# Where tiles begin in their partition: small working tiles moved to a pool at the end

## The chip, the core and the metric

The kernel runs on one core of one Trainium2 chip. TensorE (PE in the rows, its weight loads PEld), VectorE (DVE), ScalarE (ACT), GpSimd (POOL) and SyncE (SP, which issues the DMAs) work side by side and wait for each other by semaphores. The metric is the device time of one execution in microseconds, the median of three runs.

## The reference

Two layers over 512 positions of width 1024, all in float32. Layer 0 mixes tokens by gated linear attention in chunks of 64, layer 1 by a short gated convolution; each is followed by a causal convolutional feed-forward network of width 2816, and a last RMS norm ends it:

```
for i in range(DEPTH):                                   # DEPTH = 2
    h = rmsnorm(x, norm_mix_g[i])
    x = x + (gla_mixer(h, ...) if i % 2 == 0 else short_conv_mixer(h, ...))
    h = rmsnorm(x, norm_ffn_g[i])
    x = x + conv_ffn(h, ...)     # up = causal_dwconv(h @ w_up); (silu(a) * u) @ w_down
return rmsnorm(x, final_norm_g)
```

## The kernel before

x lies transposed in SBUF: eight tiles of 128 channels by 512 positions. To keep float32 accuracy every large product is three matmuls of float32r parts (`mm3`, L176 to L181): each operand is split into a rounded high part and the rest as a low part, and high by high, high by low and low by high are added in PSUM. One matmul keeps a 128x128 block as its stationary operand, which a weight load brings in, and streams the other, moving, operand of 128x512 past it. Mostly the weights are stationary (`wh`, `wl`, split from the loaded `wr`) and the activations move (`xh`, `xl` for a layer's input, `g0h` to `g21l` for the feed-forward's middle). For v (`v_unit`, L345) it is the other way: the weights move and blocks of `xh`, `xl` are stationary. The last output tile is done in halves of 256 positions (`dn7a`, `dn7b`), with its weights split into tiles that the layer's input has left (`wlast`).

Weights come in 201 units of up to 512 KB; each is loaded (L85), its high part is copied by ScalarE (L105), its low part is subtracted by VectorE (L106), and TensorE takes it in the order of the program. Nothing is scheduled by a planner: each engine runs its instructions in program order.

Tiles lie in pools, one pool behind the other in every partition, in the order in which the pools are opened (L38 to L42): const, wraw, wsp, work, big. Within a pool the tiles lie in the order in which they are first made, and a tile smaller than 32 bytes takes 32 (`rl0` and `rl1` take 64 each, for two buffers). Starts are counted in bytes from the beginning of the partition:

| tiles | first start before | rest after division by 512 |
|---|---|---|
| `ident`, `onesr`, `causal` (const) | 35328 | 0 |
| `wr`; `wh`, `wl` (wraw, wsp) | 36864; 53248 | 0 |
| `acc`, `sq` (also `sh`, `sl`), `r`, `u` (work) | 77824 | 0 |
| `ends`, `wst` (work, 8 and 3 numbers, made in `decays`) | 94208 | 0 to 160 |
| `c1`, `c0` (work) | 94400 | 192 |
| `rl0`, `rl1` (work, 2 numbers) | 102592 | 192, 256 |
| all of big: `als`, `xh`, `xl`, `g*`, `y*`, `s*`, `v`, `qs`, `ks`, `zw`, `alr`, `wlast`, ... | 102720 | 320 |

The tiles of big are 2048 bytes each, so all of them have rest 320; so have their blocks of 128 columns, which are 512 bytes. The small tiles ahead of them are what sets that rest.

## Time and profile before

| | |
|---|---|
| median of 3 runs | 1128.9 us (1128.77 to 1128.91) |
| the profiled execution | 1128.92 us, of it 1127.2 us from the first instruction to the last |
| TensorE busy | 1117.7 us, 5020 matmul records |
| VectorE, ScalarE busy | 681.5 us, 459.7 us |
| mean granted TensorE clock | 0.998 |

The duration of one matmul in the profile (near 0.39 us for 512 columns) is from its start to the end of its results and overlaps the next one's. What a matmul costs in a stream is the distance from its start to the next start. The chain of waits gives that well: it lists stretches of work by start, length and number of instructions, and length by number is the distance.

### The profile page before, as it was taken

To read this page: it belongs to the slowest core of one execution; us is meant where nothing else is said; L and a number is where in the kernel's file an instruction comes from. 1 tells how busy PE (TensorE), PEld (TensorE's weight loads), DVE (VectorE), ACT (ScalarE), POOL (GpSimd) and SP (SyncE) were. 2 spreads that over 40 slices of the span, in tenths; PEclk is the share of its full clock that TensorE was granted. 3 is DMA by queue.
4 is the path that set the end of the run, shared out by engine and by line. 5 is a ranking of instruction groups with operands and counts; after the bars stand their busy time and mean duration, and the time that the engine had idled before them with its cause. 6 is when DMAs were issued, how large, how long until landed. Compare 5 with 4: busy or idle time off the path is not lost.

```text
span 1127.2 us, 12505 instructions
## 1 busy us (share of the span) xinstructions
PE 1117.7 (99%) x5020; PEld 922.1 (82%) x5020; DVE 681.5 (60%) x854; ACT 459.7 (41%) x610; POOL 5.1 (0%) x18
## 2 busy tenths in 40 slices
PE   9999999999999999999999999999999999999997
PEld 7888888888888888888888888888888888888887
DVE  6864675597777777433336555558777777753232
ACT  6565664354444444322232222334444444432241
POOL 1000000000000000000000000000000000000000
PEclk9999999999999999999999999999999999999999
DMA  7231223222333333233333322222333323232312
GB/s 256 76 108 61 66 65 113 94 94 94 94 95 100 102 97 89 84 103 98 95 101 99 98 94 94 94 94 94 95 101 104 94 94 94 89 101 87 97 58 75
DMA packets 33183, 108.14 MB, mean 96 GB/s; under 512 B 3619, under 2 KB 6435, under 8 KB 33125
## 3 DMA queue, kind: packets, MB, share of 16 engines
q1 hardware_dynamic: 33124, 107.34, 30.3%
q8 instruction: 39, 0.64, 0.2%
q14 instruction: 20, 0.16, 0.0%
HBM read 105.23 MB, written 2.10 MB: 95 GB/s over the span
## 4 chain that ended last, share of the span: by engine, by line
PE 99%; DVE 0%; DMA 0%; ACT 0%; SPq 0%; issue 0%; DVEq 0%
PE up L181 43%; PE dn L181 20%; PE v L181 4%; PE g L181 4%; PE scb L181 4%; PE scc L181 4%; PE so L181 4%; PE go L181 4%; PE scu L181 4%; PE k L181 2%; PE q L181 2%; PE dn7b L181 1%; PE dn7a L181 1%; PE o L402 1%; PE o L404 0%; DMA x<-in_xT 0%
## 5 line engine op out<-in xcount | busy, mean ns | idle before, releaser
L105 ACT CAST wh<-wr 128x1024 fp32r<-128x1024 f32 (+3 forms) x201 | 204.8, 1019 | 381.8 <-PE dn L181 114.5
L106 DVE TENSOR_TENSOR wl<-wr,wh 128x1024 fp32r<-128x1024 f32 (+3 forms) x201 | 237.9, 1184 | 159.9 <-ACT wh L105 155.7
L181 PE MATMUL up<-xh,wh 128*128 128x512 f32 x704 | 277.5, 394 | 0.0
L181 PE MATMUL up<-xh,wl 128*128 128x512 f32 x704 | 276.0, 392 | 0.0
L181 PE MATMUL up<-xl,wh 128*128 128x512 f32 x704 | 273.3, 388 | 0.0
L181 PEld LDWEIGHTS up<-xh,wl 128*128 128x128 f32 x704 | 132.2, 188 | 30.9
L181 PEld LDWEIGHTS up<-xl,wh 128*128 128x128 f32 x704 | 132.2, 188 | 29.4
L181 PEld LDWEIGHTS up<-xh,wh 128*128 128x128 f32 x704 | 132.5, 188 | 26.3
L494 DVE TENSOR_TENSOR u<-up,r 128x512 f32<-128x512 f32 x88 | 60.2, 688 | 75.7 <-PE up L181 75.7
L242 DVE SCALAR_TENSOR_TENSOR c<-u,ffcw,c 128x510 f32<-128x510 f32 x88 | 65.8, 750 | 2.8
L241 DVE SCALAR_TENSOR_TENSOR c<-u,ffcw,c 128x511 f32<-128x511 f32 x88 | 65.4, 746 | 0.8 <-ACT c L240 0.8
L240 ACT ACTIVATE c<-u,ffcw 128x512 f32<-128x512 f32 x88 | 63.3, 723 | 2.5 <-DVE u L494 2.1
L496 ACT ACTIVATE c<-c 128x512 f32<-128x512 f32 x44 | 27.8, 632 | 83.6 <-DVE c L242 83.6
L497 DVE TENSOR_TENSOR c<-c,c 128x512 f32<-128x512 f32 x44 | 30.5, 693 | 1.6 <-ACT c L496 0.2
L234 DVE RECIPROCAL r<-r 128x512 f32<-128x512 f32 x8 | 26.8, 3351 | 4.7 <-ACT r L233 4.7
L217 ACT ACTIVATE sq<-x 128x512 f32<-128x512 f32 x34 | 21.0, 623 | 12.6 <-DVE x L531 10.9
L181 PE MATMUL g<-xh,wh 128*128 128x512 f32 x64 | 25.9, 404 | 0.0
L181 PE MATMUL v<-wh,xh 128*128 128x512 f32 x64 | 25.7, 401 | 0.0
L207 DVE SCALAR_TENSOR_TENSOR xl<-x,small,xh 128x512 fp32r<-128x512 f32 x32 | 23.6, 746 | 3.2 <-ACT xh L206 3.1
L181 PE MATMUL v<-wl,xh 128*128 128x512 f32 x64 | 25.3, 396 | 0.0
L181 PE MATMUL v<-wh,xl 128*128 128x512 f32 x64 | 25.3, 396 | 0.0
L181 PE MATMUL scu<-xh,wh 128*128 128x512 f32 x64 | 25.2, 394 | 0.0
(798 smaller groups left out, 1864.2 us busy)
## 6 DMA issues: line engine op xcount, KB each, us to landing
wr<-in_w_up SPq DMA_DIRECT2D x88, 512.0 KB, 3.4
wr<-in_w_dn SPq DMA_DIRECT2D x32, 512.0 KB, 3.5
wr<-in_w_sc SPq DMA_DIRECT2D x24, 512.0 KB, 3.3
wr<-in_w_dn SPq DMA_DIRECT2D x16, 384.0 KB, 3.1
wr<-in_w_v SPq DMA_DIRECT2D x8, 512.0 KB, 3.4
wr<-in_w_g SPq DMA_DIRECT2D x8, 512.0 KB, 3.3
wr<-in_w_go SPq DMA_DIRECT2D x8, 512.0 KB, 3.4
wr<-in_w_so SPq DMA_DIRECT2D x8, 512.0 KB, 3.4
```

The lines of the kernel that those rows point to most:

```text
L105: S.copy(hh, r[:, c:e])
L106: V.tensor_sub(ll, r[:, c:e], hh.bitcast(F32))
L181: PE.matmul(out, lhsT=a, rhs=b, start=first and i == 0, stop=last and i == 2)
L207: V.scalar_tensor_tensor(l, x[k], col(gi, k), h.bitcast(F32), op0=ALU.mult, op1=ALU.subtract)
L217: S.activation(sq, x[k], AF.Square)
L234: V.reciprocal(r, r)
L240: S.activation(c, u, AF.Copy, scale=cw[:, 2:3])
L241: V.scalar_tensor_tensor(c[:, 1:], u[:, :T - 1], cw[:, 1:2], c[:, 1:], op0=ALU.mult, op1=ALU.add)
L242: V.scalar_tensor_tensor(c[:, 2:], u[:, :T - 2], cw[:, 0:1], c[:, 2:], op0=ALU.mult, op1=ALU.add)
L494: V.tensor_mul(u, ups[i], r)
L496: S.activation(cs[0], cs[0], AF.Silu)
L497: V.tensor_mul(cs[1], cs[1], cs[0])
```

## The change

The tiles `ends`, `wst`, `rl0` and `rl1` are made in a pool of their own, `tiny`, which is opened behind big. Nothing else differs.

```
     big = ctx.enter_context(tc.tile_pool(name="big", bufs=1))
+    tiny = ctx.enter_context(tc.tile_pool(name="tiny", bufs=2))
...
-    def wk(name, shape=(P, T), dt=F32, bufs=2, tag=None):
-        return work.tile(list(shape), dt, tag=tag or name, name=name, bufs=bufs)
+    def wk(name, shape=(P, T), dt=F32, bufs=2, tag=None, pool=work):
+        return pool.tile(list(shape), dt, tag=tag or name, name=name, bufs=bufs)
+    def tk(name, shape, bufs=2):
+        return wk(name, shape, bufs=bufs, pool=tiny)
...
-        ends = wk("ends", (P, NPAIR, 2))
+        ends = tk("ends", (P, NPAIR, 2))
...
-        wst[h] = wk("wst", (P, NPAIR - 1), bufs=4)
+        wst[h] = tk("wst", (P, NPAIR - 1), bufs=4)
...
-        rt = wk(f"rl{th}", (P, 2))
+        rt = tk(f"rl{th}", (P, 2))
```

In the program that is built from it, `c1` and `c0` begin at 94208 and big at 102400, so that every tile of big has rest 0 instead of 320; `ends`, `wst` and `rl` lie from 225280 on. `const`, `wraw`, `wsp` and `acc` to `u` stay where they are. Of what matmuls read, `ones` (one column, at 16544, rest 160) and `rl` still do not begin at a multiple of 512. Every engine has the same instructions in the same order with the same waits as before; only addresses differ.

## Rows read from the trace of the kernel before

**Rows 1.** Page: busy time by engine; the chain that ended last, by engine.
```profile
PE 1117.7 (99%) x5020; PEld 922.1 (82%) x5020; DVE 681.5 (60%) x854; ACT 459.7 (41%) x610; POOL 5.1 (0%) x18
...
PE 99%; DVE 0%; DMA 0%; ACT 0%; SPq 0%; issue 0%; DVEq 0%
```

**Rows 2.** Waits of TensorE: for whom, us in total, times, longest.
```profile
PE warm L68 <- DVE warm L56: 1.5, 1, 1.5
PE sums L552 <- DVE sq L546: 1.0, 1, 1.0
PE rb L565 <- DVE rl L559: 0.6, 1, 0.6
```

**Rows 3.** Busy time and granted clock in one stretch of the feed-forward's first product.
```profile
225.00:455.00 230.00, 230.00 (x1006) 188.80 (x1006) 171.34 (x214) 101.74 (x131) 0.00 (x0) 1.00 0.30 95
```

**Rows 4.** Chain of waits: start us, us, what; weights stationary, activations moving.
```profile
16.27 10.99 PE q L181 x48
...
169.60 43.95 PE go L181 x192
...
225.00 230.73 PE up L181 x1008
455.73 120.85 PE dn L181 x528
...
576.58 5.49 PE scc L181 x24
```

**Rows 5.** The same chain: v, first and last stretch, with weights moving and activations stationary.
```profile
56.33 22.39 PE v L181 x96
...
104.14 5.60 PE v L181 x24
```

**Rows 6.** The same chain: sums of squares, `sh`, `sl` moving, `onesr` stationary.
```profile
27.26 0.46 PE sums L231 x2
...
103.68 0.47 PE sums L231 x2
...
763.83 0.46 PE sums L231 x2
```

**Rows 7.** The same chain: low-rank gate, `als` stationary, `xh`, `xl` moving.
```profile
10.08 0.45 PE al L262 x2
...
11.22 0.45 PE al L262 x2
...
13.53 0.46 PE al L262 x2
...
14.68 0.45 PE al L262 x2
```

**Rows 8.** The same chain: the last output tile's halves, 256 columns, `wlast` stationary.
```profile
1100.77 7.90 PE dn7a L181 x66
...
1113.96 3.60 PE dn7b L181 x30
```

**Rows 9.** The same chain: the four products for the keys.
```profile
33.21 5.50 PE k L181 x24
...
38.95 5.59 PE k L181 x24
...
44.77 5.51 PE k L181 x24
...
50.51 5.59 PE k L181 x24
```

**Rows 10.** The same chain: float32 matmuls of 256 columns, for the states.
```profile
85.53 0.86 PE kva L386 x4
```

**Rows 11.** Page, costliest groups: two VectorE products of the same shape.
```profile
L494 DVE TENSOR_TENSOR u<-up,r 128x512 f32<-128x512 f32 x88 | 60.2, 688 | 75.7 <-PE up L181 75.7
...
L497 DVE TENSOR_TENSOR c<-c,c 128x512 f32<-128x512 f32 x44 | 30.5, 693 | 1.6 <-ACT c L496 0.2
```

## The prediction

> **What bounds the kernel now.** I read the page's busy times and its chain first. TensorE is busy for 1117.7 of 1127.2 us, and the chain that ended last is TensorE for 99% [rows 1]. The waits of TensorE come next: the three that matter add up to 3.1 us, one at the start and two at the tail [rows 2], so no other engine, queue or transfer sets the pace between. [...] So only one thing can move this time by much: the distance from one matmul's start to the next.

> The chain of waits gives that distance, as length by number. In the products with stationary weights it is 230.73 us / 1008 = 228.9 ns, and the same in 120.85 / 528, in 43.95 / 192, in 10.99 / 48 and in 5.49 / 24 [rows 4]. A column seems to take one cycle: the last tile's 120.0 ns for 256 columns and the gate's 226.3 ns for 512 [rows 7, 8] are 106.3 ns apart, and 256 cycles at 2.4 GHz are 106.7. By that 512 columns are 213.3 ns, and 15.6 ns of every matmul are something else. In v it is 22.39 / 96 = 233.2 ns, and 5.60 / 24 = 233.3 in the last of its five stretches [rows 5]. There are then at least two paces for the same shape, and what differs between these stages is which operand begins at which rest modulo 512 (and in which pool it lies). With the table of starts:

> - moving 320, stationary 0 (most of the kernel): 228.9 ns [rows 4];
> - moving 0, stationary 320 (v): 233.2 ns [rows 5];
> - moving 0, stationary 0 (sums): eight pairs, five of 0.46 and three of 0.47 us, 3.71 / 16 = 231.9 ns [rows 6];
> - moving 320, stationary 320 (the gate): 0.45, 0.45, 0.46 and 0.45 us for pairs, 1.81 / 8 = 226.3 ns [rows 7]; and the last tile's halves, 256 columns, 7.90 / 66 = 119.7 and 3.60 / 30 = 120.0 ns [rows 8], which is 13.3 ns over 256 cycles.

> **The change part by part.** It removes, adds and moves no instruction, DMA or wait. What it does is this: in the 4374 matmuls with stationary weights the moving operand goes from rest 320 to 0 while the weights stay at 0; in the 192 of v and in few others the stationary one goes from 320 to 0 while the moving one stays at 0; the gate, the attention's own products and the last tile go from both 320 to both 0. The 4374 are up 2112, dn 990, go and so 192 each, the short convolution 576, g 192, q 72 from 16.27 us on, and the two products for keys that run at 5.50 and 5.51 us [rows 9].

> For both at 0 in a long stream no row of before exists, so the price is bounded from both sides. The nearest rows by operands are the sums, 231.9 ns, but each is a pair in the middle of another stage's stream. The nearest by relation are the gate and the last tile: there both operands begin at the same rest, as they will everywhere after. If the rest matters because a weight load reads while the matmul before it still streams, the relation of the two starts should count and not the rest itself; both at 0 is then like both at 320. The halves give 120.0 ns for 256 columns, and 256 columns more at 2.4 GHz add 106.7, so 226.7 ns for 512; the gate gives 226.3. Two different stages with this relation give one pace, and it is below both others. I take 226.6.

> The sum: 4374 x (228.9 - 226.6) = 10.1 us; v 192 x (233.2 - 226.6) = 1.3 us; the two slow products for keys [rows 9], 48 x (232.9 - 226.6) = 0.3 us; sums 16 x 5.3 = 0.1 us. Together 11.7 us off the profiled execution's 1128.92 us (its span of 1127.2 and 1.7 us around it), which agrees with the median of 1128.9: **1117.2 us**.

> What else the addresses touch costs nothing on the path. VectorE writes `u`, at rest 0, in 688 ns and `c`, at rest 192, in 693 ns by the same kind of product [rows 11], so a start changes such an instruction by 5 ns at most, and VectorE has 59 us to spare in 230 [rows 3]. If that cover went, 88 + 44 such instructions at 5 ns would be 0.7 us. A TensorE that is 1% faster asks for 171.34 us of VectorE in 228 instead of 230, so no new wait comes of it. In the tail the tiles of 2 numbers move, in single instructions that wait for semaphores (1.6 us in two waits [rows 2]); I count zero, and some 0.1 us either way.

> The rows show 13 to 20 ns per matmul over 512 cycles, whatever the starts. [...]

> **The rivals.**

> *The pace belongs to a moving operand at rest 0, and it is the slow one.* Place: all 4374 matmuls. Both stages that move from rest 0 are slow, v over 192 matmuls at 233.2 and the sums at 231.9 although their stationary operand is at 0 too [rows 5, 6]; none of them shows 226. If this is right the kernel gets slower by 4374 x 4.3 = 18.8 us at v's pace, or 4374 x 3.0 - 192 x 1.3 = 12.9 us at that of the sums: 1147.7 or 1141.8 us. It decides as soon as the steady pace after is above 229.4 ns (0.2% of the time). Against it: the keys' second and fourth products run at 5.59 / 24 = 232.9 ns with the moving operand at 320 and the weights at 0, the first and third with the same rests at 229.2 and 229.6 [rows 9], so a slow pace does not need a moving operand at 0.

> *The rest modulo 512 is not what counts.* These same rows [rows 9] say that one set of starts has two paces, which a stretch keeps once it has fallen into one. Then the stages differ by history, or by the region of SBUF that they read (all tiles with rest 0 lie below 94208, all of big above 102720, so rows of before cannot part rest and region), and a shift of 320 bytes does nothing. 320 and 0 are both multiples of 64 bytes. The time is 1128.9 us; if v alone falls to 228.9 it is 192 x 4.3 = 0.8 us less, 1128.1. Against it: v is slow from the first of its stretches to the last [rows 5], up keeps 228.9 through 1008 matmuls on end [rows 4].
> [...]

> *Both at 0 removes the whole overhead.* The nearest row without it is that of float32 states, 0.86 / 4 = 215 ns for a record of 256 columns [rows 10]. At 215 ns the sum is 4374 x 13.9 + 192 x 18.2 + 48 x 17.9 = 65.2 us, 1063.7 us. Against it: the sums have both at 0 and no 215 among them [rows 6].

> **How the numbers follow.** Equal starts at some 226.6 ns: 0.34, with 1112 to 1122 us as its own range (225.5 to 227.6 ns). A larger gain, down to 1063.7: 0.10. No effect: 0.24. A moving operand at 0 is slow, 1133 to 1149 us: 0.32. This kernel's runs tell 0.2%, or 2.3 us, from no change. So faster 0.44, same 0.24, slower 0.32, and the range goes from 1110 to 1149 us: it leaves out the larger gain and little above. It is wide because cases of both signs hold it, and the rows part them only by a few short stretches.

> **What would show it.** After the change the chain of waits should have up x1008 at about 228.4 us instead of 230.73, dn x528 at 119.6, and v at 21.8 per 96, the same pace in all stages. If up shows 234 to 235 us, the moving operand at 0 is the slow case; if up and v both keep their lengths, the rest does not count; up below 225 us means more than the relation of starts. New waits of TensorE, or another length of VectorE's products, would mean that I have missed a part. The prediction is wrong if the pace in up is not between 225.5 and 227.6 ns.

## The result: 1117.5 us, and the profile after

The changed kernel takes 1117.5 us in the median (1117.2 to 1117.8 in four runs), the kernel before beside it 1128.8 us (1128.6 to 1128.9): a ratio of 0.990, with a 95% interval of 0.988 to 0.992. A second set of runs gave 1117.6 us and 0.989 (0.988 to 0.991). The forecast was 1117.2 us, faster. The profiled execution took 1117.47 us, 11.45 less than that of before; its span is 1115.8 us.

Busy time by engine, from the page of the kernel after, answers to [rows 1]:

```profile
PE 1106.3 (99%) x5020; PEld 920.9 (83%) x5020; DVE 682.1 (61%) x854; ACT 461.0 (41%) x610; POOL 5.0 (0%) x18
```

TensorE lost 11.4 us, and the number of its instructions is the same; VectorE and ScalarE did what they did before. The waits of TensorE are those of [rows 2], with the same lengths:

```profile
PE warm L73 <- DVE warm L61: 1.5, 1, 1.5
PE sums L557 <- DVE sq L551: 1.0, 1, 1.0
PE rb L570 <- DVE rl L564: 0.6, 1, 0.6
```

So the time went into no wait and came out of none. The stretch of the first feed-forward product, with the columns of [rows 3] (busy time of PE, PEld, DVE, ACT and POOL, each with its count, then granted clock, DMA share and GB/s):

```profile
222.20:450.00 227.80, 227.80 (x1007) 188.63 (x1006) 171.12 (x214) 102.27 (x131) 0.00 (x0) 1.00 0.29 96
```

TensorE is busy throughout at a granted clock of 1.00, as before [rows 3]. The chain of waits of the kernel after (start us, us, what) answers to [rows 4] with its up and dn rows, to [rows 9] with k (the first two of four equal rows), to [rows 5] with v, to [rows 6] with sums, to [rows 8] with the last tile:

```profile
32.90 5.44 PE k L186 x24
...
38.57 5.44 PE k L186 x24
...
55.57 21.76 PE v L186 x96
...
101.90 0.45 PE sums L236 x2
...
102.35 5.46 PE v L186 x24
...
222.11 228.48 PE up L186 x1008
450.59 119.68 PE dn L186 x528
...
1089.34 7.91 PE dn7a L186 x66
...
1102.54 3.59 PE dn7b L186 x30
```

Every long stretch of 512 columns now has one pace: 228.48 / 1008 = 119.68 / 528 = 21.76 / 96 = 226.7 ns. Short stretches behind the work of another stage take a little longer, as v's last does with 5.46 / 24 = 227.5 ns. What was at 228.9 came down by 2.2 ns, v by 6.5, the keys' two slow products by 6.2; the last tile, whose operands already began alike, kept its 119.8 ns per 256 columns. Added up by stage from the two chains: up 4.7 us, dn 2.2, the short convolution 1.3, v 1.2, go and so 0.9, k 0.4, g 0.4, q 0.2, sums 0.1, and 0.1 at the start. Within the rounding that is all of the 11.45 us.

### The profile page after: what moved, and what is told of

The parts are those of the page before. It is cut to its first block, busy times and chain, and to the rows that moved or that the text cites. A ratio compares the mean times of both kernels' runs of the same rounds, so it can differ in the third digit from the quotient of the medians.

```text
span 1115.8 us, 12505 instructions
## 1 busy us (share of the span) xinstructions
PE 1106.3 (99%) x5020; PEld 920.9 (83%) x5020; DVE 682.1 (61%) x854; ACT 461.0 (41%) x610; POOL 5.0 (0%) x18
## 4 chain that ended last, share of the span: by engine, by line
PE 99%; DMA 0%; DVE 0%; ACT 0%; SPq 0%; issue 0%; DVEq 0%
PE up L186 43%; PE dn L186 20%; PE g L186 4%; PE v L186 4%; PE scb L186 4%; PE scu L186 4%; PE scc L186 4%; PE go L186 4%; PE so L186 4%; PE k L186 2%; PE q L186 2%; PE dn7b L186 1%; PE dn7a L186 1%; PE o L407 1%; PE o L409 0%; DMA x<-in_xT 0%
## 5 line engine op out<-in xcount | busy, mean ns | idle before, releaser
L186 PE MATMUL up<-xh,wh 128*128 128x512 f32 x704 | 273.9, 389 | 0.0
L186 PE MATMUL g<-xh,wl 128*128 128x512 f32 x64 | 25.0, 390 | 0.0
```

The costliest lines, as they stand in the source:

```text
L186: PE.matmul(out, lhsT=a, rhs=b, start=first and i == 0, stop=last and i == 2)
```

## Experiments

Three questions stood open. Is it the relation of the two starts that counts, or the moving operand's own start, or the region of SBUF (theories: relation, operand, region or history)? Over what modulus? And which part of the change is needed? The edits of the kernel are pads: an unused tile ahead of a pool, which shifts all that lies behind it.

**Everything at 320.** After, with 320 bytes ahead of the split weights' pool: weights and activations all begin at 320.

```diff
+    ctx.enter_context(tc.tile_pool(name="pad0", bufs=1)).tile([P, 80], F32, name="pad0")
     wsp = ctx.enter_context(tc.tile_pool(name="wsp", bufs=3))
```

> The changed kernel with a pad of 320 bytes ahead of the weights' tiles: wh, wl, the working tiles and big all begin at rest 320, so the relation of moving and stationary start is 0 as after the change, but nothing is a multiple of 512. If the relation of the two starts counts: up x1008 at 228.5 us (226.7 ns), time 1117 to 1118 us. If each operand has to begin at a multiple of 512: at least the 228.9 ns of before, 1128 us or more. If only history or region counts: a pace of 226.7, 228.9 or 233 that cannot be told beforehand.

1117.58 us beside 1128.76 of before. The chain of this kernel:

```profile
55.47 21.76 PE v L187 x96
...
222.13 228.50 PE up L187 x1008
```

These are the lengths of after, with no tile of a large matmul at a multiple of 512. That tells for the relation and against the multiple.

**Weights at 320, activations at 0.** The same pad, and 192 bytes ahead of the working tiles.

```diff
+    ctx.enter_context(tc.tile_pool(name="pad0", bufs=1)).tile([P, 80], F32, name="pad0")
     wsp = ctx.enter_context(tc.tile_pool(name="wsp", bufs=3))
+    ctx.enter_context(tc.tile_pool(name="pad1", bufs=1)).tile([P, 48], F32, name="pad1")
     work = ctx.enter_context(tc.tile_pool(name="work", bufs=2))
```

> The changed kernel with 320 bytes ahead of the weights' tiles and 192 more behind them: stationary weights at rest 320, moving activations at 0, the reverse of before; in v the weights move from 320 and the blocks at 0 are stationary. If the relation counts, up goes at the 233.3 ns that v had before (235 us for 1008), v at the 228.9 ns that up had (21.97 us for 96), time 1117.5 + 4374 x 6.65 ns + 192 x 2.2 ns = 1147 us. If a slow pace comes of the moving operand alone (it is at 0 here as in the changed kernel): no change, 1117.5. If region or history: no change either, or no pattern between up and v.

1147.75 us beside 1128.76: with the same activations at 0 as in after the kernel is 30 us slower, so a moving operand at 0 is neither fast nor slow by itself. The chain of this kernel, and its window over up:

```profile
56.66 22.40 PE v L188 x96
...
96.93 5.51 PE v L188 x24
...
226.88 235.19 PE up L188 x1008
```
```profile
226.88:462.07 235.19, 235.19 (x1009) 189.81 (x1009) 172.37 (x214) 101.13 (x132) 0.00 (x0) 1.00 0.29 93
```

up takes v's old pace, 233.3 ns, with TensorE busy to the last and the clock at 1.00, as the exchange of the two relations asks. But v, which has up's old starts in exchange (moving 320, stationary 0) and was expected at 21.97 us, shows 233.3 ns over 96 products and 229.6 in three of its four later stretches: what was expected of v did not come out. At this relation there are two steady paces, as the keys' rows of before had it [rows 9].

**All pairs in steps of 64 bytes.** The products alone, with the rest of the computation left out: 64 pairs of starts, 48 products each, in one order and then in the reverse.

```diff
+    for s in steps:
+        for d in steps:
+            stretch("a", d, s)
+    for d in reversed(steps):
+        for s in reversed(steps):
+            stretch("b", d, s)
```

> Matmuls alone, nothing of the reference is computed (x is copied to the output): 48 for each of 64 pairs of starts, moving rest d and stationary rest s in steps of 64 bytes, from two tiles whose bases are multiples of 512, all pairs in one order and then in the reverse order. If the relation counts: the pace is a function of (d - s) mod 512 alone, 226.7 ns on the diagonal, 228.9 at d - s = 320 (up of before), 233.3 at 192 (v of before), the same in both orders. If own alignment counts: fast only in row s = 0 and column d = 0, or at their crossing. If history counts: the two orders differ for the same pair. If region counts: one pace everywhere.

The chain of this kernel; a name has the order (a, b), the moving start after m, the stationary one after s:

```profile
21.58 10.88 PE am0s0x L56 x48
32.46 11.00 PE am64s0x L56 x48
43.47 11.15 PE am128s0x L56 x48
54.62 11.20 PE am192s0x L56 x48
...
76.72 11.00 PE am320s0x L56 x48
...
464.22 11.20 PE am0s320x L56 x48
...
519.68 10.90 PE am320s320x L56 x48
...
1371.46 11.20 PE bm0s320x L56 x48
```

All 128 stretches fall into four lengths by one number, the moving start less the stationary one, modulo 256: at 0 they take 10.88 to 10.92 us per 48 (227 ns), at 64 10.99 to 11.01 (229), at 128 11.14 to 11.16 (232), at 192 11.19 to 11.21 (233). Before's up is 320 - 0, that is 64; its v is 0 - 320, that is 192. All these tiles lie in the lowest 56 KB of their partitions, and the order makes no difference: neither region nor history is needed for the paces of before's up and v. The second pace that one relation showed above does not appear in these stretches of 48.

**Large activations 256 and 128 bytes on.** After, with the pad ahead of `big`: the modulus and the size at half of it, in the kernel.

```diff
+    ctx.enter_context(tc.tile_pool(name="pad0", bufs=1)).tile([P, 64], F32, name="pad0")
     big = ctx.enter_context(tc.tile_pool(name="big", bufs=1))
```

> The changed kernel with 256 bytes ahead of big: activations at rest 256, weights at 0. The grid repeats after 256 bytes, so by it up x1008 stays at 228.5 us and the time at 1117.5. If a multiple of 512 is what it takes, as the change has it: slower, 1128 us or more.

1117.64 us beside 1128.84, and up as in after:

```profile
222.07 228.48 PE up L187 x1008
```

So 256 is enough in the kernel too. With 32 elements in place of 64 the shift is 128 bytes:

> The changed kernel with 128 bytes ahead of big. By the grid (128 apart: 232.2 ns) up x1008 is 234.1 us, v the same pace, and the time 1117.5 + 4566 x 5.5 ns = 1142.6 us. If a multiple of 64 or 128 is enough: 1117.5.

1147.36 us, 5 us above the figure expected. The chain of this kernel:

```profile
57.15 22.30 PE v L187 x96
...
215.43 11.16 PE up L187 x48
226.59 0.46 PE sums L237 x2
227.05 235.20 PE up L187 x1008
...
585.45 5.60 PE scc L187 x24
...
602.68 5.57 PE scc L187 x24
```

v has the grid's pace, 232.3 ns, up 233.3. The direction came out and the size did not: up and dn at 1.1 ns more than the grid's 232.2 make 3.3 of the 5 us. The grid's short stretches give the fast pace exactly, but away from it one relation has more than one steady pace. In this chain the pace changes where another stage's matmuls stand between: up runs at 232.5 ns ahead of a pair of sums and at 233.3 behind it, the short convolution at 233.3 ahead of the next pair and at 232.1 behind. In the rows of before, the keys' pace changes behind each single product z that stands between them (5.50 and 5.59 us in turn [rows 9]), but the same pair of sums leaves up at 229 ns. Why a stretch takes the one pace or the other is open.

The single distances from start to start in the traces show what such a pace is. In up of after every distance is 226 or 227 ns. In up of before they go round through about 226, 229 and 232 ns, and 228.9 is their mean. The keys' second product of before, with the same starts, stays at 233 and 234 ns nearly throughout. So one set of starts has two patterns here, and a pace is the mean over one of them.

**Finer steps, and whose load meets the stream.** The products alone again: moving starts in steps of 4 bytes against a stationary one at 0, equal starts at 4 to 60, and alternating starts, which should tell whether a product's stationary start counts against its own moving start or against that of the product before.

```diff
+    for d in range(0, 260, 4):
+        stretch("f", d, 0)
+    for e in (4, 16, 32, 48, 60):
+        stretch("e", e, e)
+    mixed("own", (0, 64), (0, 64))
+    mixed("cross", (0, 64), (64, 0))
+    mixed("owna", (0, 128), (0, 128))
+    mixed("crossa", (0, 128), (128, 0))
...
```

> Matmuls alone again, nothing of the reference is computed. First the stationary operand at 0 and the moving one at 0 to 256 in steps of 4 bytes, 48 matmuls each. If lines of 64 bytes count, the pace is flat over 64 bytes and steps at 64, 128, 192; if lines of 16, it has a step every 16 bytes; if the start itself, it rises evenly, and below 226.7 may lie somewhere just under 256. Then both at 4, 16, 32, 48, 60: 226.7 if the difference alone counts. Then starts that alternate from one matmul to the next by 64 (and by 128): own = each matmul's two operands at the same rest, cross = each matmul's moving operand at the same rest as the NEXT matmul's stationary one. If the weight load that runs beside the stream counts, cross is at 226.7 and own at about 231 (232.2 for 128); if a matmul's own two operands count, the reverse. Last 256 columns at a difference of 0, 64, 128, 192: 120.0 at 0, and the same steps if the loss is one per weight load.

```profile
20.95 10.88 PE fm0s0x L56 x48
31.83 11.32 PE fm4s0x L56 x48
...
76.51 11.52 PE fm20s0x L56 x48
...
199.79 11.00 PE fm64s0x L56 x48
...
750.04 11.46 PE em4s4x L56 x48
761.50 11.04 PE em16s16x L56 x48
772.54 10.92 PE em32s32x L56 x48
...
805.63 22.24 PE ownm0s0x L65 x96
827.87 22.23 PE crossm0s64x L65 x96
850.10 21.92 PE ownam0s0x L65 x96
872.02 22.08 PE crossam0s128x L65 x96
```

In the chain of this kernel 0 is the fastest step (226.7 ns; 256 has the same with the entry), 64 the next kind (229), 4 bytes off cost 235.8 and 20 bytes 240. The pace is not flat over 16 or 64 bytes and does not rise evenly, so none of the three expectations for the steps came out. Equal starts are not enough: both at 4 run at 238.8 ns, both at 16 at 230.0, both at 32 at 227.5 with the entry into the stretch. The two streams that alternate by 64, expected at 226.7 and about 231 ns in one order or the other, run alike, at 231.7 and 231.6. Those that alternate by 128, expected at 226.7 and 232.2, run at 228.3 (own) and 230.0 (cross). Neither theory had that, and whose load it is stays open.

**Before, with 192 bytes ahead of `big` and nothing else.** The small tiles stay in their pool.

```diff
+    ctx.enter_context(tc.tile_pool(name="pad0", bufs=1)).tile([P, 48], F32, name="pad0")
     big = ctx.enter_context(tc.tile_pool(name="big", bufs=1))
```

> The kernel before, with 192 bytes of padding ahead of big and nothing else: ends, wst and rl stay in the middle of work, c1 and c0 stay at rest 192, big goes from 320 to 0 (modulo 512). If the start of big is all that the change did: 1117.5 us and up x1008 at 228.5. If moving the small tiles or c1, c0 did a part of it: more than 1118.

1119.17 us in one run beside 1129.5 (1128.9 to 1130.3). Its chain:

```profile
4.10 5.90 DMA x<-in_xT
...
34.09 5.44 PE k L182 x24
...
223.31 228.48 PE up L182 x1008
...
1110.26 1.24 PE rb L566 x4
```

up is after's to the hundredth, so the start of `big` is what the change did to the matmuls, and the pool for small tiles is only its means. The time is above the 1118 us that the expectation set as a sign of more. The extra 1.6 us lie in two places: the chain begins with a later load of `x`, so that k starts at 34.09 us instead of 32.90, and rb takes 1.24 us instead of 0.72. Both occur with the small tiles in their new pool too: the shift by 128 has a load of `x` that ends later still, and rb takes 1.24 us in the profiled run of the faster tail below. So these rows do not charge them to the small tiles, and one run cannot tell more.

**A faster tail.** The last tile's weights moved 64 bytes on, since products of 256 columns in the finer steps' kernel were fastest at a difference of 192 (10.89 us per 96, 11.51 at 0). It was measured beside the second set of after.

```diff
-            [bt(f"x{2 * i + j}{hl}", f"wlast{i}{j}{hl}", (P, T), F32R) for hl in "hl"] for j in range(2)]
+            [bt(f"x{2 * i + j}{hl}", f"wlast{i}{j}{hl}", (P, T + 64), F32R)[:, 16:16 + T] for hl in "hl"] for j in range(2)]
```

> The changed kernel, with the last weights (wlast) 64 bytes into their tiles (and these 256 bytes longer, so that the others keep their rest modulo 256). The fine grid gave 256 columns 113.3 ns with the moving start 192 bytes after the stationary one modulo 256 and 120.0 with equal starts. If that holds in the kernel: dn7a x66 at 7.5 us instead of 7.91, 132 x 6.7 ns = 0.9 us less, 1116.6 us. If the tail's order by three terms and its waits take it back: 1117.5.

> The changed kernel once more, beside the next one: 1117.5 us.

1117.71 us (1116.99 to 1118.03) against 1117.60 (1117.29 to 1117.81) for after: no difference that can be told. The chain of the shifted kernel:

```profile
1089.69 7.78 PE dn7a L186 x66
...
1102.69 3.42 PE dn7b L186 x30
```

These two stretches lost 0.13 and 0.17 us, where 66 and 30 matmuls at 6.7 ns less would be 0.44 and 0.20, and no version here beats the changed kernel.

**Other column counts.** The products alone: 128 to 512 columns at four differences, and three alternating streams.

```diff
+    for cols in (128, 192, 256, 320, 384, 448, 512):
+        for d in (0, 64, 128, 192):
+            mixed(f"c{cols}q", (d,), (0,), cols=cols)
+    mixed("alts", (0,), (0, 64))
+    mixed("altm", (0, 64), (0,))
+    mixed("seq", (0, 0, 64, 64), (0, 0, 64, 64))
```

> Matmuls alone, nothing of the reference is computed: 72 each of 128 to 512 columns at differences of 0, 64, 128, 192. If the loss at equal starts is one per weight load: columns / 2.4 + 13.3 ns, 384 at 173.3, 448 at 200.0. If it is one cycle in 17 of the stream: 170.0 and 198.3, and 256 columns at 113.3, which equal starts did not show. Last, starts that alternate: stationary 0 and 64 under moving 0 (differences 0 and 192), moving 0 and 64 over stationary 0 (0 and 64), and both in pairs 0, 0, 64, 64: if the difference decides matmul by matmul, 230.0, 227.8 and 226.7 to 229; if a steady state over many matmuls is needed, other values.

Rows of its chain; the number after c is the columns:

```profile
85.56 8.65 PE c256qm0s0x L65 x72
...
111.23 8.19 PE c256qm192s0x L65 x72
119.42 10.55 PE c320qm0s0x L65 x72
...
161.65 12.51 PE c384qm0s0x L65 x72
...
270.25 16.36 PE c512qm0s0x L65 x72
...
336.64 16.59 PE altsm0s0x L65 x72
353.23 16.62 PE altmm0s0x L65 x72
369.85 16.72 PE seqm0s0x L65 x72
```

At equal starts 256, 384 and 512 columns take 120.1, 173.8 and 227.2 ns, the entry into the stretch included: 53.6 and 53.5 ns for each 128 columns more, that is 0.418 ns a column, and on the same line 13.1 ns at no columns. At 256 columns the order of the differences is another, 192 being the fastest (113.8 ns), and at 320 all four take 146.5 to 146.7 ns, so there these differences do not count. The stream with alternating weights has 230.4 ns, near the mean of the two relations in it (226.7 and 233.3); the one with alternating moving starts has 230.8, where that mean is 227.8, and a stream in blocks of two has 232.2 instead of 227 to 229. Two misses, then, for a sum by each product's own relation. Some counts do not fit the line either: 448 columns take 202.5 ns at equal starts and 200.1 at 64, and 128 and 192 columns take 111 to 112 ns at every difference.

## Why the prediction was right

**The bound.** TensorE's start-to-start distance was the only thing that could move the time much, and it did: the stretches shrank, the waits did not [rows 2], and VectorE still has 57 us to spare in 228 (171.12 us of work in 227.80).

**The mechanism.** The step that decided was to read the gate and the last tile [rows 7, 8] as "both start alike" and not as "both start at 320". That is shown by everything at 320 (1117.58 us), by weights at 320 (1147.75) and by the grid. What the prediction left out is the modulus: it is 256, so 512 is more than is needed. Nor is every equal start enough: 32 and the multiples of 64 bytes gave the fast pace (226.7 to 227.5 ns), 4, 16, 48 and 60 did not (230.0 to 238.8 ns).

The prediction gave this case 0.34 and the opposite one, a slow moving operand at 0, 0.32. Its range, 1110 to 1149 us, held the measured times of every version of the kernel here, the slowest too. So the rows of before had not decided the sign; the mechanism was right as the somewhat likelier of two.

**The sizes.** 226.6 ns was taken and 226.7 measured, so the large term measured 9.7 us instead of 10.1; v gave 1.2 (1.3), the keys' two slow products 0.3 (0.3), the sums 0.1 (0.1). The 120.0 ns of the last tile plus 106.7 for 256 columns more was the better of the two sources; 0.45 us for a pair, read to 10 ns, could not have told 226 from 229. The profile gives the granted clock as a share of full speed, 1.00 in both stages, and no run shows it in GHz: the 2.4 of the prediction is a rate of columns, estimated from the 106.3 ns between 256 and 512 of them [rows 7, 8], which is 2.41 a ns. In the kernel of other column counts that step is 107.1 ns (120.1 to 227.2), or 2.39 a ns. That the sum with this step came out is partly luck. It holds at equal starts, but at differences of 64, 128 and 192 the kernels of products alone have 117.8, 118.6 and 113.4 ns for 256 columns, which with 107.1 gives 224.9, 225.7 and 220.5, where 512 columns take 229, 232 and 233.

The price of VectorE's starts was misread, without effect on the sum: `c` begins at rest 0 in after and its product still takes 692 ns beside 688 for `u`, so the 5 ns between them [rows 11] are not a matter of their starts.

**The rival of a moving operand at 0.** Its best witnesses, the sums at 231.9 ns with both at 0 [rows 6], fell: they show 0.45 us a pair now. They are pairs inside a stream of another relation, and streams that alternate starts run at 228 to 232 ns in the two experiments that have them. A pair's length there tells of its neighbours too. The gate's pairs, on which the prediction leaned, are of the same kind and read 0.45 to 0.47 us in after; that the one witness pointed right and the other wrong was luck. v was slow for its difference of 192, 233 ns in the grid at every moving start, not for its 0.

**The rival of no effect.** Its ground, one set of starts with two paces [rows 9], is real: weights at 320 and the shift by 128 show it again. But no run here shows a second pace at the fast relation in a long stretch of 512 columns. In after all four products for the keys take 5.44 us, and the 16 grid stretches at equal starts, like all others at difference 0, take 10.88 to 10.92 us per 48. That 320 and 0 are both multiples of 64 bytes did not make them alike: starts 64 apart cost 229 ns against 226.7 in the grid.

**The rival of the whole overhead.** 226.7 ns is 13.3 above the prediction's 213.3, an estimate from the column rate in [rows 7, 8], and 12.5 above 512 columns at the 0.418 ns of the last experiment (214.2). Equal starts took away 2.2 of before's 15.6 ns and nothing here took away the rest.

**What is shown and what is argued.** That the pace of 512 columns depends on the difference of both starts, at multiples of 64 bytes, is shown: 226.7, 229, 232 and 233 ns in the grid. The traces also show a weight load beside the stream: in up of before and of after a load takes 0.19 us and starts 2 to 5 ns behind the start of the matmul ahead of its own. That the pace differs because these two reads meet was my guess from that; no run shows it. What the runs show is 226.7 against 233.3 ns for the same instructions at other starts. Why the period is 256 bytes is open, and so is what sets the second pace.

## What to carry to other kernels

Where TensorE is the bound, divide the chain's long stretches by their counts, and put the pace beside the starts of both operands: two paces for one shape, here 228.9 and 233.2 ns, are a hint that addresses matter. For products of 512 columns let both kinds of operands begin alike modulo 256, at a multiple of 64 bytes (226.7 ns here, 229 to 233 at the other differences); for other widths measure first, since 256, 320 and 448 columns do not follow the same order. A pool of odd-sized small tiles ahead of the large ones can spoil this for all of them (1128.8 us here), and one pad brings it back (1119.2 us with 192 bytes). Price such a thing from long uniform stretches: pairs amid another stage's work measure the mixture.
